# Making the low part of every second weight block with an adding DMA, in a decoder trunk in split float32

## The chip, the cores and the metric

The kernel runs on one core of a Trainium2 chip. The metric is the device time of one execution in microseconds. The core has TensorE (PE, the matrix engine, with its weight loads shown as PEld), VectorE (DVE), ScalarE (ACT), GpSimd (POOL), SyncE (SP, used here to issue loads) and 16 DMA engines. The kernel before takes 2185.58 us (median of three runs, 2185.21 to 2185.61).

## The reference

A trunk of two layers on 256 positions with 2048 channels, all in float32. Every weight matrix is used once.

```
x = x + ConformerConv(RMSNorm(x))        # 2048->4096, gate, 31-tap depthwise conv, LayerNorm, SiLU, 2048->2048
x = x + SwiGLU(RMSNorm(x))               # 2048->5632 twice (gate, up), 5632->2048 (down)
k, v = RMSNorm(x) @ w_k, RMSNorm(x) @ w_v
x = x + W_o DilatedAttention(RMSNorm(x) @ w_q, k, v)   # 16 heads, three dilated windows
x = x + SwiGLU(RMSNorm(x))
out = RMSNorm(x)
```

## The kernel before, in words

**Two parts for each number.** The matrix products run on operands of type float32r, a form of float32 that keeps fewer bits. To keep accuracy, an operand is split: the high part is the number as float32r, the low part is what is left (the number minus the high part). A product is then three products: high x high, high x low and low x high. For activations both parts lie side by side in one tile (`x[:, kt, 0, :]` and `x[:, kt, 1, :]`), so that one 512-wide matmul with the high part of a weight makes the first two; a 256-wide one with the low part of the weight makes the third.

**Blocks.** All weights come as blocks of 512 KB (128 partitions x 1024 float32), in the order in which they are used. The list `blocks` is made at the start (lines 120 to 147): the first convolution matrix gives 64 blocks, the second 32, each feed-forward 176 for gate and up and 88 for down, the value matrix 32, and key, query and output 32 each, 752 in all. The first block of the first feed-forward has index 96.

`emit_block` (line 153) writes the code that loads and splits the next block: a DMA from SP's queue into a tile `raw` (line 173; `RAW` = 4 buffers), an ACT copy that rounds it to the high part `whi` (line 176), and a subtraction raw - high into the low part `wlo` (line 178). The subtraction is DVE's, except for most blocks of the first convolution matrix and three of the second, where it is POOL's. `whi` and `wlo` have `AHEAD` + 1 = 3 buffers each. A few blocks of the convolution (`native`) are used unsplit, as float32, from a tile `rawn`.

`next_block` (line 183) is called where a block is about to be used; it first calls `emit_block` until the block used now and the next `AHEAD` = 2 are written. The order in which each engine runs its instructions is then fixed when the program is built, by a scheduler that goes by the order of the code and by readiness; in one stretch (line 579, `manual_schedule`) ACT, DVE and POOL keep the order of the code.

**How blocks are used.** `project` (line 236) goes through the blocks of 256 output channels, four blocks for a matrix of 2048 rows and eleven for the first down matrix. For each, `block` (line 213) runs eight wide matmuls (line 217: high weight, both parts of the activation, 512 columns) and eight narrow ones (line 222: low weight, high activation, 256 columns). The order of the two alternates: the first block of a projection runs wide first, the next narrow first, the third wide first, and so on (`narrow_first`). `project_nat` (line 288; values and the last down matrix) has the weight as the moving operand: twelve 512-wide matmuls a block, in threes of high, low, high (lines 303 to 305); for the very last part it holds three blocks at once.

**Stages.** First the convolution (`project_mixed`, line 245, and `conv`), in which DVE, ACT and POOL also do the 31 taps. `stats` (line 528) squares each finished channel group for the layernorm; most squares are added up on POOL, the first and the last three have tiles of their own. Then the layernorm and the second convolution matrix (`project_pair`, lines 576 to 632), the first feed-forward (`ffn_hidden`, line 636, and `out_proj`, line 391), keys, values and attention, and the second feed-forward.

In a feed-forward, 22 units each use four blocks of gate and four of up. After a projection ACT and DVE collect the result (`collect`, lines 326 and 327); POOL multiplies it by the norm's scale twice, before and after ACT's SiLU (lines 643 to 645); at the end of the unit DVE multiplies (line 647), ACT makes the high part of the hidden value (line 648) and POOL its low part (line 649). POOL also sums squares for the next norm (line 355).

Of the kernel before, what the change touches and what calls it, by code (L numbers as in the profile page):

```python
# [9 lines left out]
F32 = mybir.dt.float32  # L10
F32R = mybir.dt.float32r
AF = mybir.ActivationFunctionType
ALU = mybir.AluOpType
# [3 lines left out]
P = 128  # L17
D = 2048
S = 256
DT = D // P  # L20
# [10 lines left out]

GK, NB = 4, 256
GKV, NBV = 2, 512
RAW, AHEAD = 4, 2
NATIVE = 4

TAPS_OF = [(6, 0)] * 14 + [(6, 6), (3, 16)]
# [36 lines left out]
def _bc(ap, n):  # L74

    return ap.unsqueeze(1).broadcast_to([ap.shape[0], n, ap.shape[1]])
# [3 lines left out]
def trunk(ctx: ExitStack, tc: tile.TileContext, xT, vec, const, w1, w2, wk, wv, wq, wo, wg0, wu0, wd0, wg1, wu1, wd1, fing, out):  # L80
    nc = tc.nc
# [16 lines left out]
    wp = ctx.enter_context(tc.tile_pool(name="wp", bufs=1))  # L98
# [10 lines left out]
    def v(name, i, n=1):  # L109
        o = _VEC[name] + i  # L110
        return vecs[:, o:o + n]
# [8 lines left out]
    blocks = []  # L120

    def plan(w, u, kt_n, gk=GK):
        blocks.extend((w, u, g, gk) for g in range(kt_n // gk))
# [9 lines left out]
    for wg, wu, wd in ((wg0, wu0, wd0), (wg1, wu1, wd1)):  # L133
        for u in range(FT // 2):
            plan(wg, u, DT)
            plan(wu, u, DT)
        if wd is wd1:
            for c in range(D // NBV):
                plan(wd, c, FT, GKV)
        else:  # L140
            for u in range(DT // 2):
                plan(wd, u, FT)
            for c in range(D // NBV):
                plan(wv, c, DT, GKV)
            for w in (wk, wq, wo):
                for u in range(DT // 2):
                    plan(w, u, DT)
    ready = []
    used = [0]
    conv_pool = []  # L150
# [2 lines left out]
    def emit_block():  # L153
        i = len(ready)
        w, u, g, gk = blocks[i]
        shape = [P, gk, GK * NB // gk]
        native = NATIVE if g == 0 and (w is w1 or w is w2 and u < 2) else 0
        if native:
            raw = conv_pool[0].tile(shape, F32, name="rawn", bufs=2)
        else:  # L160
            raw = wp.tile(shape, F32, name="raw", bufs=RAW)
        hi = lo = None
        if native < gk:
            hi = wp.tile(shape, F32R, name="whi", bufs=AHEAD + 1)
            lo = wp.tile(shape, F32R, name="wlo", bufs=AHEAD + 1)
        src = w[u, g].rearrange("p (k n) -> p k n", k=gk)
        with_x = w is w1 and u == 0
        step = gk if not with_x else 1 if g == 0 else 2
        for s in range(0, gk, step):
            if with_x:  # L170
                load_x(GK * g + s, step)
            part = slice(s, s + step)
            nc.sync.dma_start(raw[:, part, :], src[:, part, :])
            part = slice(max(s, native), s + step)
            if part.start < part.stop:
                nc.scalar.copy(hi[:, part, :], raw[:, part, :])  # L176
                eng = nc.gpsimd if (w is w1 and u > 1) or (w is w2 and u < 2 and (u, g) in ((0, 1), (1, 1), (0, 2))) else nc.vector
                eng.tensor_tensor(out=lo[:, part, :], in0=raw[:, part, :], in1=hi[:, part, :].bitcast(F32), op=ALU.subtract)  # L178
        ready.append((raw, hi, lo))
        if with_x and g == DT // GK - 1:  # L180
            x_loaded()

    def next_block(w, u, g, ahead=AHEAD):
        i = used[0]
        used[0] += 1
        assert blocks[i][:3] == (w, u, g)
        while len(ready) < min(len(blocks), i + 1 + ahead):
            emit_block()
        return ready[i]

# [45 lines left out]
    def project(w, u, kt_n, x):  # L236

        bk = bank2()
        for g in range(kt_n // GK):
            hi, lo = next_block(w, u, g)[1:]  # L240
            block(bk, x, hi, lo, [(g * GK + j, j, m, slice(m * P, (m + 1) * P)) for j in range(GK) for m in range(2)], kt_n)
            tick()
        return bk
# [162 lines left out]
    with tc.tile_pool(name="cv", bufs=1) as cv, tc.tile_pool(name="cvu", bufs=1) as cvu:  # L406
# [11 lines left out]
        def load_x(kt, n):  # L418
            nc.sync.dma_start(hT[:, kt:kt + n, :], xT[:, kt:kt + n, :])
            for j in range(kt, kt + n):  # L420
                if j < NATIVE:
                    nc.vector.tensor_scalar(out=xf[:, j, :], in0=hT[:, j, :], scalar1=v("a_g", j), scalar2=None, op0=ALU.mult)
                else:
                    split_scaled(x, j, v("a_g", j))

        def x_loaded():
            nc.sync.dma_start(cst, const)
            nc.sync.dma_start(vecs[:, 3 * DT:], vec[:, 3 * DT:])
            for j in range(0, DT, 2):
                norm.add(hT[:, j:j + 2, :], *((nc.gpsimd, nc.gpsimd) if j < 4 else (nc.scalar, nc.vector)))  # L430

        shift = None
# [93 lines left out]
        sqa = []  # L526

        def stats(j):

            if j in (0, DT - 3, DT - 2, DT - 1):  # L530
                sq = cv.tile([P, S], F32, name=f"sq{j}", bufs=1)
                nc.scalar.activation(sq, cT[:, j, :], AF.Square)
                if j == 0:
                    sqa.append(sq)
            else:
                sq = cv.tile([P, S], F32, name="sq", bufs=2)
                nc.scalar.activation(sq, cT[:, j, :], AF.Square)
                nc.gpsimd.tensor_tensor(out=sqa[0], in0=sqa[0], in1=sq, op=ALU.add)
            nc.tensor.matmul(st[:, 0, :], ones, cT[:, j, :], start=j == 0, stop=j == DT - 1, skip_group_check=True)
            if j == DT - 3:  # L540
                nc.tensor.matmul(st[:, 1, :], ones, sqa[0], start=False, stop=False, skip_group_check=True)
            if j >= DT - 3:
                nc.tensor.matmul(st[:, 1, :], ones, sq, start=False, stop=j == DT - 1, skip_group_check=True)
# [24 lines left out]
        for _ in range(3):  # L568
            emit_block()


        for j in left:
            stats(j)
# [3 lines left out]
        bks = [bank2(), bank2()]  # L577
        pair = project_pair(w2, cT, z, bks)
        with tc.manual_schedule(engines={mybir.EngineType.Activation, mybir.EngineType.DVE, mybir.EngineType.Pool}):
            mu = cv.tile([P, S], F32, name="mu")  # L580
            rl = sp.tile([P, S], F32, name="rstd")
            groups = [(0, 1), (1, 1)] + [(j, 2) for j in range(2, DT, 2)]

            def centred(j, n, eng, m):
                c2 = cT[:, j:j + n, :]
                eng.tensor_tensor(out=c2, in0=c2, in1=_bc(m, n), op=ALU.subtract)

            def scaled(j, n):

                c2 = cT[:, j:j + n, :]  # L590
                nc.vector.tensor_tensor(out=c2, in0=c2, in1=_bc(st[:, 1, :], n), op=ALU.mult)
                for q in range(j, j + n):
                    nc.scalar.activation(cT[:, q, :], cT[:, q, :], AF.Silu, bias=v("ln_b", q), scale=v("ln_g", q))

            def parted(j, n):
                nc.vector.tensor_copy(z[:, j:j + n, 0, :], cT[:, j:j + n, :])
                nc.vector.tensor_tensor(out=z[:, j:j + n, 1, :], in0=cT[:, j:j + n, :], in1=z[:, j:j + n, 0, :].bitcast(F32), op=ALU.subtract)


            nc.scalar.activation(rl, st[:, 0, :], AF.Square)  # L600
            nc.scalar.copy(mu, st[:, 0, :])
            centred(*groups[0], nc.vector, st[:, 0, :])
            nc.vector.tensor_tensor(out=rl, in0=st[:, 1, :], in1=rl, op=ALU.subtract)
            nc.scalar.activation(rl, rl, AF.Sqrt, bias=ln_eps)
            centred(*groups[1], nc.vector, st[:, 0, :])
            for j, n in groups[5:]:
                centred(j, n, nc.gpsimd, mu)
            nc.vector.reciprocal(st[:, 1, :], rl)
            for i, (j, n) in enumerate(groups):
                if 2 <= i < 5:  # L610
                    centred(j, n, nc.vector, st[:, 0, :])
                scaled(j, n)
                if j in (1, 2):
                    next(pair)
                if j >= 8:
                    parted(j - 4, 2)
                if j == 10:
                    next(pair)
                    next(pair)
            emit_block()  # L620
            parted(12, 2)
            next(pair)
            parted(14, 2)
            next(pair)
            emit_block()
            emit_block()
            next(pair)
            next(pair)
            parted(0, 2)
            parted(2, 2)  # L630
# [26 lines left out]
    with tc.tile_pool(name="at", bufs=1) as ap:  # L657
# [46 lines left out]
        for c in range(D // NBV):  # L704
            bk = project_nat(wv, c, x)
            for t in range(2):
                nc.scalar.activation(vn[:, t, c * NBV:(c + 1) * NBV], bk[t], AF.Identity,
                                     scale=norm.rn[:, t:t + 1])
# [121 lines left out]
```

## Time and profile before

| | |
|---|---|
| median of 3 runs | 2185.58 us |
| profiled execution, whole | 2185.62 us |
| its span, first to last instruction | 2183.8 us |
| mean granted clock of TensorE | 0.997 |
| busy: PE, DVE, ACT, POOL | 99%, 63%, 49%, 21% |
| read from HBM | 398.28 MB |
| DMA share of SP's queue | 55.4% of the 16 engines' span |

The profile is of one execution. Rows of instructions name the line, the engine, the operation, the tile written and the tiles read, then how often, the busy time, the mean duration of one in nanoseconds, and the idle time of the engine before them with what ended it. Busy times of PE are a union, since matmuls overlap; a single matmul's duration is longer than the distance between two. A row of the waits reads: engine and line, what it waited for, the total in us, how often, the longest. A row of the timeline or the chain begins with the time since the start of the span and a duration. DMA is the mean busy share of the 16 DMA engines.

### The profile page before, as it was taken

The page shows a single profiled execution, that of the slowest core. Times are in us where ns is not written, and L with a number is a line of the kernel's source. Part 1 is how long each engine was busy: PE and PEld are TensorE (multiplying, and loading weights), DVE is VectorE, ACT ScalarE, POOL GpSimd, SP SyncE. Part 2 cuts the span into 40 slices and gives each one's busy share as a digit, 9 for nine tenths or more (in the row PEclk, how much of TensorE's full clock was granted, in tenths as well). Part 3 has the DMA queues.
Part 4 walks back from the last instruction along what each step waited for, and adds up shares of the span by engine and source line. Part 5 has one row for each costly group of instructions (what it writes and reads, how often), then busy time and mean ns, then how long its engine had stood idle before and what let it go on. Part 6 is the DMA issues. An engine that isn't in the chain of part 4 may idle for free.

```text
span 2183.8 us, 31131 instructions
## 1 busy us (share of the span) xinstructions
PE 2165.4 (99%) x12254; PEld 1904.9 (87%) x12254; DVE 1368.0 (63%) x1636; ACT 1062.1 (49%) x1385; POOL 452.2 (21%) x284
## 2 busy tenths in 40 slices
PE   9999899999999999999999999999999999999998
PEld 8999788888888888888888888888888888888887
DVE  7888776656665654555545677766566665655554
ACT  6665545444444444444444566554444444453333
POOL 5998112122222220000000100112222222210000
PEclk9999999999999999999999999999999999999999
DMA  7454255555556565555555544555555555555654
GB/s 256 166 174 165 98 192 183 193 193 188 189 186 191 185 193 191 193 187 189 183 194 190 188 146 143 185 183 187 192 185 190 191 193 192 186 194 193 194 193 160
DMA packets 112899, 402.42 MB, mean 184 GB/s; under 512 B 12656, under 2 KB 13680, under 8 KB 112752
## 3 DMA queue, kind: packets, MB, share of 16 engines
q1 hardware_dynamic: 111456, 398.30, 55.4%
q8 instruction: 96, 1.57, 0.3%
q10 hardware_dynamic: 1296, 2.12, 0.3%
q14 instruction: 51, 0.42, 0.1%
HBM read 398.28 MB, written 2.10 MB: 183 GB/s over the span
## 4 chain that ended last, share of the span: by engine, by line
PE 97%; DVE 1%; ACT 0%; issue 0%; DMA 0%; SPq 0%; POOL 0%; ACTq 0%; DVEq 0%
PE pp L217 47%; PE pp L222 25%; PE pp L259 8%; PE pp L304 4%; PE pp L303 4%; PE pp L305 4%; PE aux L305 1%; PE aux L304 1%; PE aux L303 1%; PE pp L284 1%; PE pp L272 0%; DVE aux L470 0%; PE aux L694 0%; PE aux L671 0%; PE pt L689 0%
## 5 line engine op out<-in xcount | busy, mean ns | idle before, releaser
L178 DVE TENSOR_TENSOR wlo<-raw,whi 128x1024 fp32r<-128x1024 f32 (+1 forms) x692 | 938.8, 1369 | 509.6 <-ACT whi L176 508.9
L176 ACT CAST whi<-raw 128x1024 fp32r<-128x1024 f32 (+1 forms) x737 | 772.3, 1048 | 793.3 <-PE pp L217 402.9
L217 PE MATMUL pp<-x,whi 128*128 128x512 f32 x3328 | 802.2, 392 | 0.0
L217 PEld LDWEIGHTS pp<-x,whi 128*128 128x128 f32 x3328 | 611.2, 188 | 117.3
L222 PEld LDWEIGHTS pp<-x,wlo 128*128 128x128 f32 x3328 | 427.0, 191 | 16.4
L222 PE MATMUL pp<-x,wlo 128*128 128x256 f32 x3328 | 433.3, 283 | 0.0
L327 DVE TENSOR_TENSOR t<-pp,t 128x512 f32<-128x512 f32 x104 | 71.9, 692 | 208.2 <-ACT t L326 208.2
L326 ACT COPY t<-pp 128x512 f32<-128x512 f32 x104 | 61.0, 586 | 259.5 <-PE pp L217 259.5
L649 POOL TENSOR_TENSOR hid<-t,hid 128x512 fp32r<-128x512 f32 x44 | 90.2, 2049 | 419.8 <-ACT hid L648 419.8
L217 PE MATMUL pp<-hid,whi 128*128 128x512 f32 x704 | 168.7, 391 | 0.0
L217 PEld LDWEIGHTS pp<-hid,whi 128*128 128x128 f32 x704 | 129.2, 188 | 24.9
L470 DVE SCALAR_TENSOR_TENSOR aux<-up,vecs,aux 128x256 f32<-128x256 f32 x350 | 140.9, 480 | 1.6 <-ACT aux L468 1.6
L355 POOL TENSOR_TENSOR sqacc<-sqacc,sq 128x512 f32<-128x512 f32 x22 | 33.0, 1502 | 513.1 <-ACT sq L351 503.4
L259 PE MATMUL pp<-x,whi 128*128 128x256 f32 x720 | 133.5, 287 | 0.0
L643 POOL TENSOR_TENSOR t<-t,rstd 128x512 f32<-128x512 f32 x44 | 57.1, 1297 | 315.6 <-DVE t L327 315.6
L259 PEld LDWEIGHTS pp<-x,whi 128*128 128x128 f32 x720 | 113.3, 192 | 0.9
L178 POOL TENSOR_TENSOR wlo<-raw,whi 128x1024 fp32r<-128x1024 f32 x45 | 107.2, 2406 | 23.0 <-ACT whi L176 23.0
L303 PE MATMUL pp<-whi,hid 128*128 128x512 f32 x264 | 103.5, 392 | 0.0
L304 PE MATMUL pp<-wlo,hid 128*128 128x512 f32 x264 | 102.9, 390 | 0.3 <-DVE wlo L178 0.3
L305 PE MATMUL pp<-whi,hid 128*128 128x512 f32 x264 | 102.8, 390 | 0.0
L259 PE MATMUL pp<-x,wlo 128*128 128x256 f32 x360 | 101.9, 283 | 0.1
L222 PEld LDWEIGHTS pp<-hid,wlo 128*128 128x128 f32 x704 | 90.8, 191 | 3.7
(156 smaller groups left out, 1987.3 us busy)
## 6 DMA issues: line engine op xcount, KB each, us to landing
raw<-wg SPq DMA_DIRECT2D x176, 512.0 KB, 3.4
raw<-wu SPq DMA_DIRECT2D x176, 512.0 KB, 4.1
raw<-wd SPq DMA_DIRECT2D x176, 512.0 KB, 3.3
raw<-w SPq DMA_DIRECT2D x75, 512.0 KB, 3.3
raw<-wv SPq DMA_DIRECT2D x32, 512.0 KB, 4.2
raw<-wk SPq DMA_DIRECT2D x32, 512.0 KB, 4.2
raw<-wq SPq DMA_DIRECT2D x32, 512.0 KB, 3.4
raw<-wo SPq DMA_DIRECT2D x32, 512.0 KB, 3.3
```

The costliest lines, as they stand in the source:

```text
L176: nc.scalar.copy(hi[:, part, :], raw[:, part, :])
L178: eng.tensor_tensor(out=lo[:, part, :], in0=raw[:, part, :], in1=hi[:, part, :].bitcast(F32), op=ALU.subtract)
L217: nc.tensor.matmul(bk[:, m, :, :], hi[:, j, ws], x[:, kt, :, :], start=kt == 0, stop=kt == kt_n - 1 and m_last, skip_group_check=True)
L222: nc.tensor.matmul(bk[:, m, 0, :], lo[:, j, ws], x[:, kt, 0, :], start=False, stop=kt == kt_n - 1 and not m_last, skip_group_check=True)
L259: nc.tensor.matmul(bks[u][:, m, :], a[:, j, m * P:(m + 1) * P], b, start=kt == 0 and m == 0 and i == 0, stop=kt == DT - 1 and i == len(pas ...
L303: nc.tensor.matmul(o, x[:, kt, 0, ts], hi[:, j, :], start=kt == 0, stop=False)
L304: nc.tensor.matmul(o, x[:, kt, 0, ts], lo[:, j, :], start=False, stop=False)
L305: nc.tensor.matmul(o, x[:, kt, 1, ts], hi[:, j, :], start=False, stop=kt == kt_n - 1)
L326: nc.scalar.copy(t, bk[:, :, 1, :])
L327: nc.vector.tensor_tensor(out=t, in0=bk[:, :, 0, :], in1=t, op=ALU.add)
L470: nc.vector.scalar_tensor_tensor(out=acc[i % 2], in0=win, scalar=w, in1=acc[i % 2], op0=ALU.mult, op1=ALU.add)
L649: nc.gpsimd.tensor_tensor(out=hid[:, 2 * u:2 * u + 2, 1, :], in0=o, in1=hid[:, 2 * u:2 * u + 2, 0, :].bitcast(F32), op=ALU.subtract)
```

## The change

From the first feed-forward on, every block with an odd index (97, 99, up to 751) gets its low part in another way: after the high part, ACT writes the negated high part into the low tile, and a DMA issued by GpSimd reads the block from HBM a second time and adds it onto that tile. All other blocks keep the subtraction. Blocks are split three ahead in place of two from there on, and `whi` and `wlo` have four buffers in place of three, throughout. To make room, `raw` has three buffers in place of four, the square of the third last channel group takes a tile of the rotating kind, and the mean of the layernorm shares the tile of the convolution's shift.

```
-RAW, AHEAD = 4, 2
+RAW, AHEAD = 3, 2
...
+    first_ff = next(i for i, b in enumerate(blocks) if b[0] is wg0)
...
+        by_dma = i > first_ff and i % 2 == 1
+        lo = None
...
-            hi = wp.tile(shape, F32R, name="whi", bufs=AHEAD + 1)
-            lo = wp.tile(shape, F32R, name="wlo", bufs=AHEAD + 1)
+            hi = wp.tile(shape, F32R, name="whi", bufs=AHEAD + 2)
+            lo = wp.tile(shape, F32R, name="wlo", bufs=AHEAD + 2)
...
                 nc.scalar.copy(hi[:, part, :], raw[:, part, :])
+                if by_dma:
+                    nc.scalar.activation(lo, hi.bitcast(F32), AF.Copy, scale=-1.0)
+                    nc.gpsimd.dma_start(lo, src, accum_op=ALU.add)
+                    continue
...
-        while len(ready) < min(len(blocks), i + 1 + ahead):
+        while len(ready) < min(len(blocks), i + 1 + ahead + (i > first_ff and ahead > 0)):
             emit_block()
...
-            if j in (0, DT - 3, DT - 2, DT - 1):
+            if j in (0, DT - 2, DT - 1):
...
-                nc.gpsimd.tensor_tensor(out=sqa[0], in0=sqa[0], in1=sq, op=ALU.add)
+                if j < DT - 3:
+                    nc.gpsimd.tensor_tensor(out=sqa[0], in0=sqa[0], in1=sq, op=ALU.add)
...
-            mu = cv.tile([P, S], F32, name="mu")
+            mu = cv.tile([P, S], F32, name="mu", tag="shift")
```

More of the change, by code (lines that the diff above doesn't have):

```diff
@@ L161, in emit_block @@
             raw = wp.tile(shape, F32, name="raw", bufs=RAW)
-        hi = lo = None
+        hi = None
         if native < gk:
-            hi = wp.tile(shape, F32R, name="whi", bufs=AHEAD + 1)
-            lo = wp.tile(shape, F32R, name="wlo", bufs=AHEAD + 1)
+            hi = wp.tile(shape, F32R, name="whi", bufs=AHEAD + 2)
+            lo = wp.tile(shape, F32R, name="wlo", bufs=AHEAD + 2)
         src = w[u, g].rearrange("p (k n) -> p k n", k=gk)
```

## The prediction

> **What bounds the kernel now.** I read the first part of the page, then the chain, then what TensorE waited for, then stretches of the span.
>
> ```profile
> PE 2165.4 (99%) x12254; PEld 1904.9 (87%) x12254; DVE 1368.0 (63%) x1636; ACT 1062.1 (49%) x1385; POOL 452.2 (21%) x284
> PE 97%; DVE 1%; ACT 0%; issue 0%; DMA 0%; SPq 0%; POOL 0%; ACTq 0%; DVEq 0%
> PE pp L272 <- ACT cT L593: 5.0, 1, 5.0
> PE pp L259 <- DMA rawn<-w: 3.7, 1, 3.7
> ...
> PE pp L304 <- DVE wlo L178: 0.3, 1, 0.3
> ```
>
> TensorE (PE) is busy 99% of the span and makes 97% of the chain that ended last. The two longest of its waits are at the start (a load) and at the layernorm (L593). For a low part made by VectorE (DVE) in the changed region it waited 0.3 us in all. So a faster subtraction has nothing to give. The stretches say the same and show DMA:
>
> ```profile
> 0.00:30.00 30.00, 25.73 (x158) 23.26 (x158) 18.64 (x32) 18.85 (x33) 4.76 (x9) 1.00 0.86 315
> 205.00:258.00 53.00, 46.83 (x245) 40.07 (x244) 43.78 (x84) 27.91 (x46) 14.50 (x10) 0.94 0.24 81
> 300.00:400.00 100.00, 100.00 (x577) 88.41 (x576) 65.31 (x60) 50.35 (x60) 18.60 (x12) 1.00 0.57 188
> 1920.00:2183.00 263.00, 256.07 (x1159) 212.02 (x1157) 133.16 (x128) 105.57 (x110) 15.78 (x9) 0.99 0.57 188
> ```
>
> After the length of a stretch come the busy times of PE, PEld, DVE, ACT, POOL, then the clock, the DMA share and GB/s. All of PE's idle time, 18.4 us, is in three places: 4.3 us at the start, 6.2 us at the layernorm, 6.9 us at the end (and about 1 us elsewhere). In the feed-forward PE has no idle time at all, and its pace does not depend on its neighbours, as the chain shows early and late:
>
> ```profile
> 258.57 3.65 PE pp L217 x16
> 264.14 3.65 PE pp L217 x16
> ...
> 1902.90 3.65 PE pp L217 x16
> 1914.04 3.65 PE pp L217 x16
> ```
>
> Sixteen wide matmuls (two blocks) take 3.65 us, and the next such group begins 5.57 us later, or twice that. So a pair of blocks costs 5.57 us: 2 x 1.83 us wide and 2 x 0.96 us narrow. That is the pace any change here must keep up with.
>
> **What the change removes.** By the code there are 752 blocks; the first of the feed-forward has index 96; odd indices after it are 97 to 751, which is 328 blocks. Each loses one DVE subtraction:
>
> ```profile
> L178 DVE TENSOR_TENSOR wlo<-raw,whi 128x1024 fp32r<-128x1024 f32 x686 | 934.7, 1375 | 509.6 <-ACT whi L176 508.9
> L176 ACT CAST whi<-raw 128x1024 fp32r<-128x1024 f32 x731 | 768.6, 1052 | 793.3 <-PE pp L217 402.9 <-PE pp L305 144.3 <-issue 140.3
> ```
>
> 328 x 1.375 = 451 us of DVE go, from 1368 to about 917, all beside PE's work: worth 0 on the path. It adds 328 ScalarE (ACT) activations of the same shape as the cast; at the cast's 1.05 us that is 345 us, taking ACT from 1062 to about 1407 us (64% of the span). ACT does not become the bound. Both are hidden; what counts is the latency of the new path.
>
> **The time the new low part has.** With four buffers of each part, block b takes the buffers of b-4. In the order of `block`, an odd block that is the second or fourth of its projection runs narrow first, so a pair is: wide odd, wide even, narrow even, narrow odd. The buffer of high part b-4 is free when its wide half ends, 0.96 + 1.83 us after its narrow half began; low part b is read two pairs after that beginning: 2 x 5.57 - 2.79 = 8.35 us. In `project_nat` a block takes 2.72 us, by the distance of two casts that wait for PE,
>
> ```profile
> 1991.48 1.05 ACT L176 CAST whi<-raw 128x1024 fp32r<-128x1024 f32 x1 [1.67 <-PE pp L305]
> 1994.20 1.05 ACT L176 CAST whi<-raw 128x1024 fp32r<-128x1024 f32 x1 [1.67 <-PE pp L305]
> ```
>
> and the low part is read one matmul (0.23 us) into its block, so the time is 3 x 2.72 + 0.23 = 8.39 us: the same. Only in every second projection of the first down matrix (11 blocks each) are odd blocks wide first; there some 22 blocks have a further 2.8 us and cost nothing. 306 are left.
>
> **What the new path takes.** One split of the kernel before gives its hops:
>
> ```profile
> 392.91 3.82 PE L217 MATMUL pp<-x,whi 128*128 128x512 f32 x16
> ...
> 396.76 1.05 ACT L176 CAST whi<-raw 128x1024 fp32r<-128x1024 f32 x1 [0.72 <-PE pp L217]
> ...
> 397.85 1.23 DVE L178 TENSOR_TENSOR wlo<-raw,whi 128x1024 fp32r<-128x1024 f32 x1 [0.54 <-ACT whi L176]
> ```
>
> At their pace the sixteen matmuls end at 392.91 + 3.65 = 396.56, and the cast that waits for them starts 0.2 us later; what waits for the cast starts 0.04 us after it. So after the buffer is free: 0.2, the cast 1.05, the negated copy 1.05 and 0.05, in sum 2.35 us. Then GpSimd (POOL) has to issue the transfer and it has to land, in 8.35 - 2.35 = 6.0 us. No POOL-issued and no adding transfer is in this trace. The nearest rows:
>
> ```profile
> L173 SPq DMA_DIRECT2D raw<-wg x176: 327/328/328, 307.4 to 1905.3; - x176
> DMA to landing us min/median/max: 3.0/3.6/7.4
> q1 hardware_dynamic: 111456, 398.30, 55.4%
> ```
>
> Issue: from SP's 0.33 us up to the longest POOL tensor operation (2.05, quoted below). I take 1.0, nearer to the SP row, since no data passes through POOL. Landing: a plain block lands in 3.0 to 7.4 us, 3.6 in the median. In 16-engine time a block costs 0.554 x 2183.8 us x 0.524 MB / 398.3 MB = 1.59 us. A transfer that adds must read the block and the tile that it adds to, so its engine time is 1 to 2 times that. I take 2, as the bytes read are doubled: landing 3.6 + 1.6 = 5.2 us. Issue and landing together are then 6.2 us, with ends of 3.3 (0.33 + 3.0) and 9.5 (2.05 + 7.4). Against 6.0 us the low part comes 0.2 us late.
>
> The Trainium skill, page "DMA: Bandwidth & Descriptors", section "Anatomy of one DMA — SWDGE (gpsimd) path", fits a GpSimd-issued DMA to 2.0 us plus its bytes over 436 GB/s. That is 3.2 us for such a block, by which the low part is 2.8 us early and the sum is the hidden case below; no run shown so far has such a transfer.
>
> **What late means.** The next odd block's chain began before the stall and gains by it, so a steady lateness is paid once in two odd blocks: 0.2 / 2 x 306 = 31 us. PE's queue is in order: the narrow half that waits holds the wide half and all later blocks behind it.
>
> **POOL's queue.** The trigger stands in POOL's in-order queue, where it was not on any path before. There it meets:
>
> ```profile
> L649 POOL TENSOR_TENSOR hid<-t,hid 128x512 fp32r<-128x512 f32 x44 | 90.2, 2049 | 419.8 <-ACT hid L648 419.8
> L645 POOL TENSOR_TENSOR t<-t,rstd 128x512 f32<-128x512 f32 x44 | 65.3, 1484 | 35.7 <-ACT t L644 35.7
> L643 POOL TENSOR_TENSOR t<-t,rstd 128x512 f32<-128x512 f32 x44 | 57.1, 1297 | 315.6 <-DVE t L327 315.6
> ...
> 401.97 1.30 POOL L643 TENSOR_TENSOR t<-t,rstd 128x512 f32<-128x512 f32 x1 [7.06 <-DVE t L327]
> 404.01 1.50 POOL L645 TENSOR_TENSOR t<-t,rstd 128x512 f32<-128x512 f32 x1 [0.74 <-ACT t L644]
> ```
>
> L643 and L645 hold POOL for 3.54 us (401.97 to 405.51) in each of 44 units. One trigger comes per 5.57 us; it falls in that stretch with 3.54/5.57 and waits half of it: 1.12 us. L649 adds 2.05/5.57 x 1.02 = 0.38. That is 1.5 us a unit, as there is no slack, or 66 us. The ends are 0 (a slack that covers it) and 4.8 us a unit, 213 us, where a trigger sits behind each of the three.
>
> **Start and layernorm.** Three raw buffers in place of four touch the start: the fourth block that needs one was loaded at 12.58, and must now wait for the first's second subtraction (14.77 + 0.68 = 15.45).
>
> ```profile
> 12.58 0.33 SPq L173 DMA_DIRECT2D raw<-w  x1
> ...
> 14.77 0.68 DVE L178 TENSOR_TENSOR wlo<-raw,whi 128x512 fp32r<-128x512 f32 x1
> ```
>
> SP's loads behind it (the last of x, the constants) wait too. That is 2.9 us later, of which PE, which reads that block only after the two before it, sees 0 to 3; I take 1. Later, three raw buffers suffice: three blocks are 1.5 pairs, 8.35 us, and less the cast and the subtraction (1.05 + 1.38) that leaves 5.9 us for a reload whose median landing is 3.6. The layernorm's shared tile and its shifted square sum keep the same operations: 0. In sum: 2185.6 (the profiled execution: span 2183.8 and 1.8 around it; the median of the runs is the same) + 1 + 31 + 66 = **2284 us**.
>
> **The rivals.** Hidden: issue and landing take under 6.0 us and leave room for POOL's queue, with POOL, ACT and DMA all beside PE. For it: the plain median is 3.6 us, so with an issue of 1 us 1.4 us are to spare if adding costs no engine time. Against it: POOL's waits of 1.3 to 3.5 us. It gives 2185.6 + 1, say 2186 us: not slower. The lateness decides, at 6.0 us.
>
> DMA-bound: in 300 to 400 us the share is 0.57, so two plain loads take 3.17 us of 5.57. A third at single price makes 4.76 (85%); at double price 6.35, more than the pair has. Then each of 328 pairs takes 0.78 us more: 2186 + 256 = 2442 us. At the best rate in the trace, 315 GB/s at 0.86 or 366 GB/s, four block-reads are 2.10 MB in 5.73 us: 2186 + 328 x 0.16 = 2238 us. Against it: with a price of up to 1.7 it fits. The Trainium skill, same page, section "Issuing engines are not separate DMA queues", says that transfers issued by the scalar, sync and gpsimd engines run on the same 16 DMA engines and interleave. By that rule the new transfers share with the loads, as this rival has it; only ACT's few and SP's are in the trace, so it is not shown for POOL here.
>
> Faster: four buffers free the layernorm's tail, where DVE's subtraction waits for PE and holds the z tiles behind it. PE's only wait there is 5.0 us, on L593, which the change doesn't touch; at most 2181 us.
>
> That the adding transfer isn't in effect can't be: the condition holds for every odd block after the first.
>
> **Chances.** Late by some tenths, with POOL's queue: 0.44 (its own range 2218 to 2391: from no queue term, 2187 + 31, to a landing 0.7 us longer, 0.35 x 306 = 107 us more). DMA-bound 0.20. Hidden 0.32. Faster 0.04. A measurement of this kernel can tell about 0.2%, 4.4 us. So faster 0.04, within 0.32, slower 0.64. The range runs from the hidden case, 2184, to the double price, 2440; beyond lie the faster case and the part of the dear ends where transfers cost over twice a load, together under 0.15.
>
> **What would show it.** Right: PE waits on a DMA into `wlo` at L222 and L304, tenths of a microsecond each, most after L643, L645 and L649; DVE about 917 us, ACT 1407 us; HBM reads 398 + 172 = 570 MB; DMA share near 85% to 100% in 300 to 400. PE's pair longer than 5.57 us by the same amount everywhere means DMA-bound, if the share is at its top. PE at 99% and 5.57 us with landings under 5 us would make it wrong on the hidden side; a landing over 7 us, on the other. A price of POOL's issue above 2 us would break the step that set it at 1.0.

## The result, and the profile after

The changed kernel takes 2474.48 us (median of four runs, 2469.09 to 2479.22) against 2185.39 us before: 1.1325 times as long, 95% interval 1.1311 to 1.1338. The prediction said 2284 us and a range up to 2440: the direction was right, the size was not. The profiled execution of the changed kernel takes 2472.4 us, its span 2470.7 us. Lines of the code move by some seven: the subtraction is now L185, the negated copy L181, the adding DMA L182, the wide matmul L224, the narrow one L229.

The first part of the page, the queues, the chain and the issues of the changed kernel:

```profile
PE 2254.0 (91%) x12254; PEld 1937.5 (78%) x12254; DVE 951.2 (38%) x1308; ACT 1383.5 (56%) x1713; POOL 688.8 (28%) x612
...
q1 hardware_dynamic: 111456, 398.30, 45.1%
q0 software_dynamic: 47232, 171.99, 40.9%
...
PE 48%; DMA 37%; ACT 8%; issue 4%; DVE 1%; POOL 1%; SPq 0%; POOLq 0%; ACTq 0%; DVEq 0%
...
raw<-wg SPq DMA_DIRECT2D x176, 512.0 KB, 5.0
...
wlo<-wg POOLq DMA_DIRECT2D x88, 512.0 KB, 7.0
wlo<-wu POOLq DMA_DIRECT2D x88, 512.0 KB, 6.8
wlo<-wd POOLq DMA_DIRECT2D x88, 512.0 KB, 7.2
```

Before, the plain loads of gate landed so:

```profile
raw<-wg SPq DMA_DIRECT2D x176, 512.0 KB, 3.4
```

DVE lost a third of its work (1368 to 951 us), and the kernel gained nothing by it. The chain that was 97% PE is now 48% PE and 37% DMA. The adds land 7 us after their issue, counted from the start of the trigger; the plain loads beside them went from 3.4 to 5.0 us. The queue rows give the price of one transfer in time of all 16 engines: a load 0.451 x 2470.7 / 760 = 1.47 us (398.30 MB are 760 blocks), an add 0.409 x 2470.7 / 328 = 3.08 us, 2.1 times as much.

What PE waited for, and the stretch from 300 to 400 us (columns as in the prediction; L311 is the matmul with the low part in `project_nat`):

```profile
PE pp L229 <- DMA wlo<-wu: 58.6, 58, 3.2
PE pp L229 <- DMA wlo<-wg: 49.9, 46, 2.6
PE pp L311 <- DMA wlo<-wd: 20.5, 22, 3.3
```

```profile
300.00:400.00 100.00, 92.31 (x506) 80.27 (x505) 42.35 (x42) 58.30 (x67) 25.96 (x24) 0.97 0.84 230
```

PE now waits for `wlo`, at the narrow half, and the clock in the stretch is 0.97 in place of 1.00. PE's idle time is 2470.7 - 2254.0 = 216.7 us, 198 more than before, and its waits for `wlo` add up to 196.5; its busy time is 89 us longer, for the same 12254 matmuls. Both together are the 287 us of the spans.

A steady stretch of the first down matrix shows the cause step by step. The timeline of PE, then ACT, then POOL:

```profile
907.32 1.22 PE L229 MATMUL pp<-hid,wlo 128*128 128x256 f32 x8 [0.66 <-DMA wlo<-wd]
908.37 3.82 PE L224 MATMUL pp<-hid,whi 128*128 128x512 f32 x16
912.03 1.11 PE L229 MATMUL pp<-hid,wlo 128*128 128x256 f32 x8
913.86 1.21 PE L229 MATMUL pp<-hid,wlo 128*128 128x256 f32 x8 [0.72 <-DMA wlo<-wd]
...
920.36 1.22 PE L229 MATMUL pp<-hid,wlo 128*128 128x256 f32 x8 [0.69 <-DMA wlo<-wd]
```

```profile
910.41 1.05 ACT L179 CAST whi<-raw 128x1024 fp32r<-128x1024 f32 x1 [3.41 <-PE pp L224]
911.50 1.06 ACT L181 ACTIVATE wlo<-whi 128x1024 fp32r<-128x1024 f32 x1
```

```profile
912.85 0.85 POOL L182 DMA_DIRECT2D wlo<-wd  x1 [5.62 <-ACT wlo L181]
```

The wide half of the odd block begins at 908.37 and ends 1.83 us later, at 910.20. The cast starts 0.2 us after that, the negated copy ends at 912.56, the trigger starts at 912.85. The narrow half that needs the result starts at 920.36, two pairs on. From buffer free to use: 10.16 us, where PE's own pace leaves 8.35. The lateness is 1.81 us, paid once in two pairs: 0.9 us a pair, and the pairs indeed are 6.54 and 6.50 us apart in place of 5.57. Over 306 pairs that is 277 us, near the whole loss.

### The profile page after: what moved, and what is told of

Its sections match the earlier page's. It is cut to its first block, busy times and chain, and to the rows that moved or that the text cites. A ratio compares the mean times of both kernels' runs of the same rounds, so it can differ in the third digit from the quotient of the medians.

```text
span 2470.7 us, 31769 instructions
## 1 busy us (share of the span) xinstructions
PE 2254.0 (91%) x12254; PEld 1937.5 (78%) x12254; DVE 951.2 (38%) x1308; ACT 1383.5 (56%) x1713; POOL 688.8 (28%) x612
## 3 DMA queue, kind: packets, MB, share of 16 engines
q1 hardware_dynamic: 111456, 398.30, 45.1%
## 4 chain that ended last, share of the span: by engine, by line
PE 48%; DMA 37%; ACT 8%; issue 4%; DVE 1%; POOL 1%; SPq 0%; POOLq 0%; ACTq 0%; DVEq 0%
PE pp L224 21%; PE pp L229 12%; DMA wlo<-wg 10%; DMA wlo<-wu 10%; DMA wlo<-wd 9%; PE pp L266 6%; ACT whi L179 4%; ACT wlo L181 3%; DMA wlo<-wk 2%; DMA wlo<-wv 2%; PE pp L311 2%; PE pp L312 2%; PE pp L310 1%; DMA wlo<-wo 1%; DMA wlo<-wq 1%
## 5 line engine op out<-in xcount | busy, mean ns | idle before, releaser
L185 DVE TENSOR_TENSOR wlo<-raw,whi 128x1024 fp32r<-128x1024 f32 (+1 forms) x364 | 508.6, 1397 | 1057.2 <-ACT whi L179 1049.8
L224 PE MATMUL pp<-x,whi 128*128 128x512 f32 x3328 | 821.5, 399 | 0.0
L224 PEld LDWEIGHTS pp<-x,whi 128*128 128x128 f32 x3328 | 625.5, 193 | 123.3
L229 PE MATMUL pp<-x,wlo 128*128 128x256 f32 x3328 | 471.3, 288 | 125.5 <-DMA wlo<-wu 58.6
L229 PEld LDWEIGHTS pp<-x,wlo 128*128 128x128 f32 x3328 | 437.2, 191 | 169.5 <-DMA wlo<-wu 71.5
L181 ACT ACTIVATE wlo<-whi 128x1024 fp32r<-128x1024 f32 x328 | 347.8, 1060 | 9.7
L182 POOL DMA_DIRECT2D wlo<-wg x88 | 76.8, 872 | 438.2 <-ACT wlo L181 214.8
L182 POOL DMA_DIRECT2D wlo<-wd x88 | 76.1, 864 | 420.6 <-ACT wlo L181 386.4
L224 PE MATMUL pp<-hid,whi 128*128 128x512 f32 x704 | 168.6, 391 | 0.0
L224 PEld LDWEIGHTS pp<-hid,whi 128*128 128x128 f32 x704 | 129.2, 188 | 24.9
L182 POOL DMA_DIRECT2D wlo<-wu x88 | 77.0, 875 | 190.3 <-ACT wlo L181 181.6
L311 PE MATMUL pp<-wlo,hid 128*128 128x512 f32 x264 | 106.4, 403 | 20.6 <-DMA wlo<-wd 20.5
L266 PEld LDWEIGHTS pp<-x,whi 128*128 128x128 f32 x720 | 113.3, 192 | 0.9
L185 POOL TENSOR_TENSOR wlo<-raw,whi 128x1024 fp32r<-128x1024 f32 x45 | 107.1, 2405 | 21.6 <-ACT whi L179 21.6
L229 PE MATMUL pp<-hid,wlo 128*128 128x256 f32 x704 | 96.1, 285 | 16.9 <-DMA wlo<-wd 16.7
L229 PEld LDWEIGHTS pp<-hid,wlo 128*128 128x128 f32 x704 | 90.9, 190 | 25.3 <-DMA wlo<-wd 22.1
L651 POOL TENSOR_TENSOR t<-t,rstd 128x512 f32<-128x512 f32 x44 | 56.7, 1288 | 188.9 <-DVE t L334 188.9
```

Of the source, the lines that this page charges most:

```text
L181: nc.scalar.activation(lo, hi.bitcast(F32), AF.Copy, scale=-1.0)
L182: nc.gpsimd.dma_start(lo, src, accum_op=ALU.add)
L224: nc.tensor.matmul(bk[:, m, :, :], hi[:, j, ws], x[:, kt, :, :], start=kt == 0, stop=kt == kt_n - 1 and m_last, skip_group_check=True)
L229: nc.tensor.matmul(bk[:, m, 0, :], lo[:, j, ws], x[:, kt, 0, :], start=False, stop=kt == kt_n - 1 and not m_last, skip_group_check=True)
L266: nc.tensor.matmul(bks[u][:, m, :], a[:, j, m * P:(m + 1) * P], b, start=kt == 0 and m == 0 and i == 0, stop=kt == DT - 1 and i == len(pas ...
L311: nc.tensor.matmul(o, x[:, kt, 0, ts], lo[:, j, :], start=False, stop=False)
```

## The experiments

Two theories stood at the start. **A, late**: the chain of split and transfer (10.2 us) is longer than its lead (8.35 us), and PE pays the difference. **B, engines full**: a pair needs 2 x 1.47 + 3.08 = 6.0 us of the 16 DMA engines, more than the 5.57 us that PE takes, whatever the lead. As a ruler for one stage I use the gate and up projections of the first feed-forward, from the last wide matmul on `z` to the first on `hid`. A row gives the shortest, median and longest duration in ns, then the start of the first and of the last in us. Before and after:

```profile
L217 PE MATMUL pp<-hid,whi x704: 389/389/398, 812.2 to 1056.1; 128*128 128x512 f32 x176
...
L217 PE MATMUL pp<-z,whi x192: 387/389/467, 254.6 to 321.3; 128*128 128x512 f32 x192
```

```profile
L224 PE MATMUL pp<-hid,whi x704: 388/389/398, 891.3 to 1156.7; 128*128 128x512 f32 x176
...
L224 PE MATMUL pp<-z,whi x192: 389/389/468, 255.8 to 322.5; 128*128 128x512 f32 x192
```

812.2 - 321.3 = 490.9 us before, 891.3 - 322.5 = 568.8 us after: 78 us lost in 88 pairs. The work ahead of it ends 1.2 us later than before.

**The DMA left out.**

```
-                    nc.gpsimd.dma_start(lo, src, accum_op=ALU.add)
```

> The changed kernel with the adding DMA left out (the low part of an odd block is then only the negated high part, so that its matmuls run on other numbers); the buffers, the three blocks ahead and ACT's second copy stay. Both theories, DMA too late for its lead (A) and DMA engines full (B): everything but the DMA is hidden, 2186 us, between 2184 and 2190. A third, that ACT's longer queue or three raw buffers cost time, gives 2200 us or more and PE waiting on ACT.

Measured: 2184.80 us, ratio 0.9999 (0.9989 to 1.0008). ACT's 328 more copies, three raw buffers, three blocks ahead and DVE's 464 us less cost and give nothing. All of the loss comes with the DMA.

**A plain copy in its place.**

```
-                    nc.gpsimd.dma_start(lo, src, accum_op=ALU.add)
+                    nc.gpsimd.dma_start(lo, src)
```

> The adding DMA becomes a plain copy of the same block from the same queue (the low part is then the whole weight). A: landing falls from 7.0 us to about 4.5, issue and landing from 7.8 to about 5.3, within the 6.0 us that are there: 2186 to 2200 us. B: a pair needs 3 x 1.47 = 4.4 us of the engines, so no bound: 2186 us. If instead GpSimd's way of issuing makes the transfer slow, whatever it does, landing stays near 7 us and the time above 2400 us.

Measured: 2236.19 us, ratio 1.0242 (1.0217 to 1.0267). Its queue and its issues:

```profile
q0 software_dynamic: 47232, 171.99, 24.1%
...
wlo<-wg POOLq DMA_DIRECT2D x88, 512.0 KB, 4.9
```

One copy takes 0.241 x 2232.0 / 328 = 1.64 us of the engines and lands in 4.9 us. So GpSimd's way of issuing is not the matter: the adding costs about twice the engine time and 2 us of landing. 51 us are left, outside A's 2200: PE still waits for a plain copy now and then.

**More lead by the low part first.** The negated high part is rounded straight from the raw block.

```
-                nc.scalar.copy(hi[:, part, :], raw[:, part, :])
                 if by_dma:
-                    nc.scalar.activation(lo, hi.bitcast(F32), AF.Copy, scale=-1.0)
+                    nc.scalar.activation(lo, raw, AF.Copy, scale=-1.0)
                     nc.gpsimd.dma_start(lo, src, accum_op=ALU.add)
+                    nc.scalar.copy(hi, raw)
                     continue
+                nc.scalar.copy(hi[:, part, :], raw[:, part, :])
```

> ACT writes the negated high part directly from the raw block, ahead of the high part. The low buffer is free 1.83 us before the high one, and the cast leaves the chain: 1.83 + 1.09 = 2.9 us more lead against a lateness of 1.8 us in a steady stretch. A: no odd block is late any more, 2186 to 2200 us. B: the engines need 2 x 1.47 + 3.08 = 6.0 us for a pair of 5.57, 0.44 us more for 328 pairs, 144 us: about 2330 us, with a DMA share of 97% or more; if the engines are already as full as they can be (93%), 2440 us or more.

Measured: 2376.50 us, ratio 1.0917 (1.0854 to 1.0981): 98 us of the loss are gone, less than A alone would give back and 46 us short of B's 2330. The adds now start earlier, the engines are at 0.97 in the first gate and up stage, and the loads land in 6.6 us in place of 5.0; in 500 to 530 us ACT's casts and negated copies wait for raw blocks by 0.2 to 2.9 us. This gives more lead and meets a second limit, the loads.

**Half the adds.**

```
-        by_dma = i > first_ff and i % 2 == 1
+        by_dma = i > first_ff and i % 4 == 1
```

> Only every fourth block (index 97, 101, ...) is added by DMA, 164 in place of 328; the rest as changed. B: a group of four blocks needs 4 x 1.47 + 3.08 = 9.0 us of the engines in 11.13: no bound, and the landing shortens with the load: 2186 to 2210 us. A: the lead is the same 8.35 us; with a landing of 5.5 to 6 us the chain takes 8.7 to 9.2 us, 0.4 to 0.8 us late in each of some 153 blocks, all paid: 2250 to 2310 us.

Measured: 2331.53 us, ratio 1.0674 (1.0656 to 1.0692). The engines are far from full, and still:

```profile
PE pp L229 <- DMA wlo<-wu: 44.0, 28, 4.4
PE pp L229 <- DMA wlo<-wg: 22.8, 19, 2.3
```

```profile
321.00:860.00 539.00, 506.06 (x2826) 441.13 (x2825) 251.00 (x202) 275.11 (x313) 143.63 (x110) 0.99 0.76 215
```

At a DMA share of 0.76 B has no reason for a loss; the adds land in 6.0 us (median, 5.1 at best), too long for the lead. A holds, though the time lies above its 2250 to 2310.

**Both cures.** Every fourth block, and the low part first by the edit above.

```
-        by_dma = i > first_ff and i % 2 == 1
+        by_dma = i > first_ff and i % 4 == 1
...
                 if by_dma:
+                    nc.scalar.activation(lo, raw, AF.Copy, scale=-1.0)
```

> Every fourth block by DMA and the negated high part written first, straight from the raw block: half the load on the engines and 2.9 us more lead. If lateness (A) and full engines (B) are all there is, each is cured: 2184 to 2192 us, no waits of PE on a DMA above some 5 us in all, PE at full clock. If some third cost (GpSimd's queue, contention of the transfers with SBUF, the clock) is behind the loss, it stays: 2230 us or more.

Measured: 2283.56 us, ratio 1.0445 (1.0419 to 1.0471). The loss is smaller and not gone, so A and B in this form were not all. POOL's timeline in this run (L654 and L658 are the operations of L653 and L657):

```profile
504.32 1.50 POOL L654 TENSOR_TENSOR t<-t,rstd 128x512 f32<-128x512 f32 x1 [0.74 <-ACT t L653]
505.91 0.88 POOL L181 DMA_DIRECT2D wlo<-wg  x1
...
515.81 1.80 POOL L658 TENSOR_TENSOR hid<-t,hid 128x512 fp32r<-128x512 f32 x1 [9.02 <-ACT hid L657]
517.56 0.85 POOL L181 DMA_DIRECT2D wlo<-wu  x1
```

Both triggers sit right behind a tensor operation. And the adds of gate land in 8.6 us, longer than with the full load.

**Lead without an earlier start.** Every block runs wide first, so a low part is read later; all 328 adds stay.

```
-        m_last = narrow_first[0] and tiles[0][0] > 0
+        m_last = False
```

> The changed kernel with every block wide first, so that a low part is read 2.8 us later against the free buffer (11.1 us in place of 8.35, against a chain of 10.2); loads, buffers and the number of adds as changed. A alone: no block late, 2186 to 2200 us. B as well: the engines' 2 x 1.47 + 3.08 = 6.0 us a pair, 144 us over, about 2330 us, as the first down matrix now runs (6.0 us a pair). With the raw loads late as in the run before, up to 2380 us. No effect of lead: 2470 us.

Measured: 2294.26 us, ratio 1.0518 (1.0477 to 1.0560): 180 of the 289 us gone with no byte less moved. The first gate and up stage:

```profile
L224 PE MATMUL pp<-hid,whi x704: 388/393/629, 827.8 to 1085.7; 128*128 128x512 f32 x176
...
L224 PE MATMUL pp<-z,whi x192: 389/392/468, 256.0 to 322.0; 128*128 128x512 f32 x192
```

```profile
322.00:827.00 505.00, 497.39 (x2824) 432.05 (x2823) 157.68 (x158) 321.00 (x356) 177.26 (x154) 1.00 0.99 275
```

505.8 us: of 78 us lost 15 are left, 5.75 us a pair, with the engines at 0.99. (The profiled execution was the longest of the four, 2312.80 us; in the run "All adds, lead everywhere" below, which treats this stage alike, it took 502.5.) That fits B, in a place behind A, and lower than the 6.0 us that I had set, since at full load a load took 0.467 x 2311.0 / 760 = 1.42 us and an add 0.420 x 2311.0 / 328 = 2.96. The stages in which the weight is the moving operand, untouched by the edit, stayed as slow as in the changed kernel (wide matmuls of the last down matrix over 212 us, before 183).

**GpSimd's queue freed.** The tensor operations of L651, L653 and L657 (the cut shows two of the three) go to DVE.

```
-            nc.gpsimd.tensor_tensor(out=t, in0=t, in1=_bc(norm.r, 2), op=ALU.mult)
+            nc.vector.tensor_tensor(out=t, in0=t, in1=_bc(norm.r, 2), op=ALU.mult)
...
-            nc.gpsimd.tensor_tensor(out=hid[:, 2 * u:2 * u + 2, 1, :], in0=o, in1=hid[:, 2 * u:2 * u + 2, 0, :].bitcast(F32),
+            nc.vector.tensor_tensor(out=hid[:, 2 * u:2 * u + 2, 1, :], in0=o, in1=hid[:, 2 * u:2 * u + 2, 0, :].bitcast(F32),
```

> The changed kernel with the three tensor operations that GpSimd has in each feed-forward unit given to DVE, which is busy 38%: in the feed-forward units the triggers have GpSimd's queue nearly to themselves. The prediction's queue term: 66 us less, about 2410 us. A and B: a trigger's wait in GpSimd's queue adds to the same lateness, but in the steady stretches without such operations the period is as long: 0 to 40 us less, 2435 to 2475 us.

Measured: 2486.16 us, ratio 1.1389 (1.1358 to 1.1421). Nothing is gained; the prediction's queue term of 66 us is not there. The adds of gate, up and down land in 7.1 to 7.3 us in place of 6.8 to 7.2.

**The raw tile as the source.**

```
-                    nc.gpsimd.dma_start(lo, src, accum_op=ALU.add)
+                    nc.gpsimd.dma_start(lo, raw, accum_op=ALU.add)
```

> The adding DMA reads the raw tile in SBUF in place of the block in HBM, so HBM reads fall back to 398 MB. If the double price is of the adding (two operands through one engine), an add still costs about 3 us of the 16 engines and lands in 6 to 7 us, 2440 us or more (raw buffers are held longer as well, which may add). If it is of HBM's second read, an add costs 1.6 us or less, lands in under 5 us, and the time is under 2300 us.

Measured: 2891.82 us (one run). Its HBM reads, queue and issues, and SP's longest wait:

```profile
q0 software_dynamic: 47232, 171.99, 30.7%
...
HBM read 398.28 MB, written 2.10 MB: 139 GB/s over the span
...
wlo<-raw POOLq DMA_DIRECT2D x328, 512.0 KB, 6.8
```

```profile
SPq L176 <- DMA wlo<-raw: 1524.5, 321, 8.8
```

Without a second read from HBM an add still takes 0.307 x 2890.0 / 328 = 2.71 us of the engines and lands in 6.8 us. By this run the price is that of adding, not of HBM. The time is worse: the raw buffer is held until the add has landed, and SP's loads wait for it, 1524.5 us in all.

**Lead and half the load.** Wide first, every fourth block; in the two matrices used as moving operand the low part is written first.

```
-        by_dma = i > first_ff and i % 2 == 1
+        by_dma = i > first_ff and i % 4 == 1
...
+                if by_dma and gk == GKV:
+                    nc.scalar.activation(lo, raw, AF.Copy, scale=-1.0)
+                    nc.gpsimd.dma_start(lo, src, accum_op=ALU.add)
+                    nc.scalar.copy(hi, raw)
+                    continue
...
-        m_last = narrow_first[0] and tiles[0][0] > 0
+        m_last = False
```

> Every fourth block by DMA, every block wide first, and in the matrices used as moving operand (values, last down matrix) the negated high part written first from the raw block. More lead everywhere without an earlier start of the transfers in the other stages, and half the load. A and B together: 2186 to 2200 us, the gate and up stage at 491 us. If it stays near the 2284 us of the run with the low part first everywhere, neither lead nor load is what that run had left.

Measured: 2210.20 us, ratio 1.0119 (1.0102 to 1.0136). The stage and the waits:

```profile
323.00:815.00 492.00, 492.00 (x2819) 432.96 (x2818) 213.97 (x202) 280.84 (x312) 139.22 (x110) 1.00 0.83 235
```

```profile
PE pp L316 <- DMA wlo<-wd: 2.8, 3, 1.4
PE pp L316 <- DMA wlo<-wv: 2.4, 4, 0.8
...
PE pp L234 <- DMA wlo<-wu: 0.6, 1, 0.6
```

In the stage PE never idles, and it takes 493.8 us, within 3 us of before. With no wait left, these 3 us are not the DMA's; they come with the order of use, which no run tested alone. What remains is a little over the expected 2200, with waits in the moving-operand matrices (L316, the low part's matmul there; L234 is the narrow half).

**The queue freed in the run with both cures.** The run with both cures, and DVE in place of GpSimd for the three operations (the cut shows the first):

```
-            nc.gpsimd.tensor_tensor(out=t, in0=t, in1=_bc(norm.r, 2), op=ALU.mult)
+            nc.vector.tensor_tensor(out=t, in0=t, in1=_bc(norm.r, 2), op=ALU.mult)
...
```

> The run with every fourth block by DMA and the low part first (2284 us), with GpSimd's three tensor operations of a feed-forward unit given to DVE. In that run each trigger in the feed-forward started the moment L654 or L658 ended. C, that this queue makes its transfers late: the gate and up stages fall from 521 us to under 500, the time to about 2235 us or less. If the transfers are late by themselves (they run beside the loads of raw): no change, 2275 to 2290 us.

Measured: 2259.15 us, ratio 1.0333 (1.0318 to 1.0349). 24 us less: GpSimd's queue does count once the engines have room. The first gate and up stage went from 521 to 513 us only, above the 500 of C, so most of what that run had left there is the late transfers themselves: those of gate still land in 8.6 us.

**All adds, lead everywhere.** The edit of "Lead and half the load", with every second block.

```
-        by_dma = i > first_ff and i % 4 == 1
+        by_dma = i > first_ff and i % 2 == 1
```

> As the changed kernel, 328 adds, with lead in every stage: wide first, and the low part first in the two matrices used as moving operand. The run with wide first alone took 2294 us; its moving-operand stages were as slow as the changed kernel's (105 and 212 us, before 88 and 183, and the last column). A: these lose most of that, some 50 us: 2235 to 2255 us. B, the engines at 99% in gate and up, holds what is left: not under 2215 us. If the moving-operand stages stay as they are, lead is not their limit.

Measured: 2278.34 us, ratio 1.0429 (1.0404 to 1.0454). The moving-operand matrices gained little (the wide matmuls of the last down matrix now over 210 us). My figure for them was wrong: by the code, the low buffer there is free only one matmul before the block's end, so writing it first saves little more than the cast's 1.05 us, and not 2.9. The load counts for more: the same matmuls run over 212 us in the changed kernel, 194 with half the adds alone and 189 with half the adds and the low part first, against 183 before.

**No adds in those matrices.** "Lead and half the load" again, with every fourth block, and adds only in the other matrices, 134 of them.

```
-        by_dma = i > first_ff and i % 4 == 1
+        by_dma = i > first_ff and i % 4 == 1 and gk == GK
```

> As the run with every fourth block and wide first (2210 us), but without adds in the two matrices used as moving operand (values, last down matrix), where that run still waited: 134 adds are left. If lead and load are the whole loss and those stages held the rest: 2186 to 2197 us. If a cost remains wherever a block is added, at most a fifth of the 25 us goes: 2203 us or more.

Measured: 2193.04 us, ratio 1.0038 (1.0024 to 1.0052). Within the expected range; no wait of PE on an add is over 0.4 us. It is the best form found with adds in it, and it is still not faster than the kernel before. The 8 us that are left are no waits for adds; the 3 us a gate and up stage of the order of use are among them.

## Why the prediction was wrong

**Nothing to gain: right.** PE at 99% with 0.3 us of waits for DVE's low parts in the region meant that 451 us less of DVE buy nothing. DVE fell by 417 us and the run without the DMA is at 0.9999.

**The lead of 8.35 us and the rule that lateness is paid once in two pairs: right.** The steady stretch shows 1.81 us late and pairs 0.93 to 0.97 us longer.

**The step that failed is the landing.** The prediction put it at 3.6 + 1.6 = 5.2 us after an issue of 1.0, a plain median plus the engine time of a second read, and so 0.2 us of lateness. Its price of two loads in engine time was right (3.08 against 1.47). In the steady stretch the trigger ends at 913.70, 1.1 us after the negated copy, so the issue was well taken; the low part is used 6.7 us later, 1.5 more than the 5.2. By the rows, which count from the start of the trigger, the adds land in 7.0 us in the median, in 6.0 at half the load, in 5.1 at best. 1.8 us late in place of 0.2 is nine times the term of 31 us: 277.

The 5.2 us are close to an add's best, 5.1. What they leave out goes with the transfers beside it: of the changed kernel's 328 adds, the 37 that began with one plain load under way landed in 5.5 us in the median, the 288 that began with two in 7.2; and the plain loads went from 3.4 to 5.0 us.

**Luck in the direction.** The row of 3.6 us counts from the start of SP's issue and holds its 0.33 us, so the sum 1.0 + 5.2 has an issue in it twice. Without it the low part would have been 0.1 us early. That the forecast had it late at all was within its rounding, and two thirds of the forecast's loss, 66 of 98 us, was the queue term, which failed too.

**The range.** The prediction's own ends for issue and landing were 3.3 and 9.5 us. From the end of the negated copy to the use it took 7.8 us, well inside. But of that upper end only 0.7 us was carried into the late case, and the range stopped at 2440.

The Trainium skill's fit (page "DMA: Bandwidth & Descriptors", section "Anatomy of one DMA — SWDGE (gpsimd) path") gives 3.2 us; here the plain copy from GpSimd's queue took 4.9 us beside the loads (3.5 at best) and the add 7.0, so the measurement decides against it, and with it the hidden case falls.

**The queue term of 66 us: wrong.** It was 0 in the changed kernel, and some 24 us where the engines had room. Why a trigger's delay costs nothing in the full case was not tested; that the transfer then meets the engines at a better moment is only an argument.

**The DMA-bound rival** gave 2442 us, close to the time, by a mechanism that does not set it. Its pair of 6.35 us was refuted by 5.75 us with the same transfers and more lead. The engines' limit lies just behind: of the 12 to 15 us that stayed lost in this stage with wide first, 3 come with the order of use, which leaves the engines 9 to 12 us in 88 pairs, some 33 to 45 us over 328. The prediction's sentence that a price of up to 1.7 loads fits does not follow from its own figures: (5.57 - 3.17) / 1.59 is 1.5.

**Start and layernorm, +1 us: too small to tell.** The work ahead of the first feed-forward ended 1.2 us later in the profiled execution; in the runs with the same start it ended between 320.8 and 322.7 us, against 321.3 before.

**Not in the prediction: the clock.** After a wait PE is not always at its old pace. PE's timeline and three stretches around one wait in the changed kernel:

```profile
424.82 1.22 PE L229 MATMUL pp<-x,wlo 128*128 128x256 f32 x8 [2.06 <-DMA wlo<-wu]
425.88 5.40 PE L224 MATMUL pp<-x,whi 128*128 128x512 f32 x16
```

```profile
424.00:426.00 2.00, 1.18 (x9) 1.18 (x10) 0.38 (x1) 0.00 (x0) 0.00 (x0) 1.00 0.82 223
426.00:430.00 4.00, 4.00 (x13) 3.13 (x12) 0.07 (x1) 0.69 (x2) 0.00 (x0) 0.57 0.97 251
430.00:432.00 2.00, 2.00 (x14) 1.80 (x13) 1.31 (x2) 1.97 (x3) 0.00 (x0) 1.00 0.40 127
```

A wait of 2.06 us is followed by 4 us at a clock of 0.57, and sixteen wide matmuls take 5.40 us in place of 3.82. Of the 89 us of longer PE busy time some 38 are of this kind: the mean clock of 0.982 over 2470.7 us stands for 44.5 us lost, the 0.997 before for 6.6. Most of the rest comes with each wait. In the steady stretch eight narrow matmuls, 0.96 us in an unbroken run, take 1.11 before a wait (912.03) and 1.05 after it (907.32 to 908.37), since overlap is lost; that is 0.24 us, and PE waits 178 times, which makes some 43 us. These parts do not simply add to the lateness: a slower PE also gives the next transfer more time. How much of it that is was not measured.

**Still open.** Why the same add lands in 5.8 to 7.1 us in the run with every fourth block and in 7.3 to 8.6 with the low part first, at nearly the same engine share, was not tested by itself. The two traces point to its start falling together with the loads': the trigger begins 1.36 us from the nearest load's start in the one and 0.59 in the other (medians), and 1.2 and 1.8 plain loads are under way on average while it lasts. The last waits of the moving-operand matrices were removed by leaving the adds out, not explained. What the clock alone costs was not tried.

## What to carry to other kernels

Relieving an engine that nobody waits for pays nothing, and the path that takes its work over gets a deadline that the old one never came near. Before moving work to a DMA, set its landing under the load that it makes itself against the lead in buffers, and remember that lateness of a few tenths repeats with every block. If the lead is short, look first at the order of use: reading the low part later took back 180 of 289 us without moving one byte less.

## What the runs showed of the hardware

- An adding DMA of 512 KB costs 2.7 to 3.1 us of the 16 DMA engines, a plain one 1.4 to 1.6 us, and it makes no great difference whether the add's source is HBM (3.08) or SBUF (2.71, one run).
- GpSimd is held 0.87 us by the trigger of an add, 0.55 by that of a plain copy.
- In the changed kernel, 129 waits of PE for an add stood at a narrow half with sixteen wide matmuls behind it. Of the 90 shorter than 1.5 us none was followed by a slowed wide group (over 4 us); of the 39 longer ones 17 were. The Trainium skill, page "TensorE: Matmul & The Clock Gate", section "Part 1: The HAM clock gate", has the clock fall after an idle window of about 3.4 us; here it also fell after single waits of about 2 us, as in the rows above.
